# A mixed attention and recurrence network on one core: the two directions of the RWKV key products share a PSUM tile and one mask operation, and ScalarE makes all block copies of the triangular inverse

## The chip, the cores and the metric

The program runs on one core of a Trainium2 chip. TensorE (PE) does the matrix products, VectorE (DVE), ScalarE (ACT) and GpSimd (POOL) the elementwise work, and SyncE (SP) issues most transfers. The metric is the device time of one execution in microseconds, lower is better.

## The reference, cut to what matters

The whole network is two blocks of several layers (attention, a recurrent layer, feed-forward layers). The change touches one branch of the recurrent layer, an RWKV recurrence that runs over 512 tokens after 256 context tokens, once forwards and once backwards, for 8 heads of width 64, and the inverse that a later gated delta rule shares with it:

```python
def wkv_scan(s0, r, decay, k, v, kk, b, reverse, emit):
    xs = tuple(jnp.moveaxis(t, 1, 0) for t in (r, decay, k, v, kk, b))
    def step(s, inp):
        r_t, w_t, k_t, v_t, kk_t, b_t = inp
        sa = jnp.einsum('bhij,bhj->bhi', s, kk_t)
        s = s * w_t[:, :, None, :] - sa[..., None] * b_t[:, :, None, :] + v_t[..., None] * k_t[:, :, None, :]
        y = jnp.einsum('bhij,bhj->bhi', s, r_t) if emit else None
        return s, y
    s_final, ys = lax.scan(step, s0, xs, reverse=reverse)
    return s_final, (jnp.moveaxis(ys, 0, 1) if emit else None)
...
    for d in range(2):
        reverse = d == 1
        s_ctx, yc = wkv_scan(s0, rc, decay_c, k_c, vc, kkc, b_c, reverse, ctx_out)
        _, yl = wkv_scan(s_ctx, r, decay_l, k_l, v, kk, b_l, reverse, True)
```

## The kernel before, in words

**Windows.** The recurrence is done in chunks of 64 tokens. A window is two chunks in each direction; there are six windows, the first two over the context (they emit nothing) and four over the 512 tokens. Each window is prepared in two halves `h` of four heads (two head pairs `pr`), so there are 12 preparations: 4 of context windows and 8 of the others ("full" ones below; `lat` in the code).

**A preparation** (`prep`) calls `decays` for direction `d` = 0 and then 1, and `products` for 0 and then 1. `decays` computes the low-rank decay and rate into a PSUM tile `mm2` (L1153), and then by a chain over ScalarE, GpSimd and VectorE (`ta`, `kd`, `G`, `EP`) the operands `KR` (L1180) and `kT` (L1184). `products` multiplies the two (L1198). `kT` holds two blocks of 64 rows for each head, so that one product gives in one half of the PSUM rows the block `N` of the triangular system, and in the other the block `AK`; the half is swapped between the directions. For full windows the same product has 128 columns, and the second 64 give `DD`. ScalarE copies `N` out, in two pieces (L1210 and L1208), VectorE multiplies `AK` by a mask over 64 rows (L1211) and `DD` by a mask over 128 rows (L1213). Four PE transposes (L1219) and a ScalarE copy (L1220) make `kn`.

**PSUM.** The pool `mm2` has one buffer of two banks. Every `decays` and every `products` takes that one tile, so each waits until the last reader of the tile before it is done. In rows of the profile this tile is called `mm`, as is the tile of the large products.

**The inverse** (`unit_inverse`) is called once for each window and once in the gated delta rule. It inverts 32 x 32 blocks by a chain of 31 pairs of VectorE operations (L1331, L1333) between stream transposes (L1321, L1336, L1337), and then joins pairs of blocks by two rounds of 32 small products (L1351, then L1353). After each round the result is copied out of PSUM in two pieces of 32 rows: the first by ScalarE (L1361), the second by VectorE (L1359).

**The steps** (`rwkv_step`, L1387 to L1440) run the recurrence itself, 12 chunks by two halves.

**What sets the order.** A scheduler puts the instructions of the whole stage in a fixed order on each engine when the program is built; each engine then works through its list in that order and waits on semaphores. The large products that feed the rest of the layer (L114 to L116, three passes of 128 x 128 by up to 512 columns) are mixed into PE's list between the small ones. An instruction of fp32 operands of the small products appears in the trace as two MATMUL rows; in the order it is one.

Of the kernel before, what the change touches and what calls it, by code (L numbers as in the profile page):

```python
# [10 lines left out]
F32 = mybir.dt.float32  # L11
F32R = mybir.dt.float32r
AF = mybir.ActivationFunctionType
OP = mybir.AluOpType
# [1072 lines left out]
def rwkv(b, I, r, dram, late, rest, conv):  # L1087
# [11 lines left out]
    nc, tc = b.nc, b.tc  # L1099
# [6 lines left out]
    with ExitStack() as es:  # L1106
        P = lambda **kw: es.enter_context(tc.tile_pool(side="left", **kw))
        cp = P(name="rw_c", bufs=1)
        w3 = P(name="rw_3", bufs=4)
# [20 lines left out]
        mask, rsc = I["k_rwmask"], I["k_rwsc"]  # L1130
# [53 lines left out]
                nc.vector.tensor_mul(kT[:, :, :, q], chunks(src, d), chunks(G, 0))  # L1184
            return kT

        def products(o, d, h, kT):
            lat = o["w"] > 1
            kr, u0 = slice(64 * d, 64 * d + 64), 64 - 64 * d
            n = 128 if lat else 64  # L1190
            KR, AK = o["KR"][h][d], o["AK"][h]
# [9 lines left out]
            pv = ps[:, :, 0:4 * n].rearrange("p q (m x t) -> p q m x t", m=4, t=64)  # L1201
            by = lambda v: v.rearrange("p (m q) t -> p q m t", q=2)
            bc = lambda mk, k: mk[:, None, None, :].to_broadcast([k, 2, 4, 64])
            ms = slice(8 * h, 8 * h + 8)
            for blk in range(2):
                rw = slice(u0 + 32 * blk, u0 + 32 * blk + 32)
                if blk:
                    nc.scalar.activation(by(o["N"][rw, ms, 0:32]), pv[rw, :, :, 0, 32:64], AF.Copy, scale=-0.5)  # L1208
                else:
                    nc.scalar.activation(by(o["N"][rw, ms]), pv[rw, :, :, 0], AF.Copy, scale=-0.5)  # L1210
            nc.vector.tensor_tensor(by(AK[kr]), pv[kr, :, :, 0], bc(mask[kr, 0], 64), op=OP.mult)  # L1211
            if lat:
                nc.vector.tensor_tensor(by(o["DD"][h][:, d]), pv[:, :, :, 1], bc(mask[:, 1 + d], 128), op=OP.mult)  # L1213
            kn = w3.tile([128, 2, 2, 128], F32, name=f"kn{d}")
            p = b.psum(512, "tr")
            for c in range(2):
                for pr in range(2):
                    m = 2 * c + pr
                    nc.tensor.transpose(p[:, m * 128:m * 128 + 128], kT[:, pr, c].rearrange("p x t -> p (x t)"), b.ident)  # L1219
            nc.scalar.activation(kn.rearrange("p c r f -> p (c r f)"), p, AF.Copy, scale=rsc[:, d:d + 1])  # L1220
            o["kn"][h].append(kn)

        def window(w):
            return {"w": w, "KR": [[], []], "kn": [[], []], "PC": [], "AK": [], "DD": [],
# [2 lines left out]
        def prep(o, h):  # L1227
            o["PC"].append(w3.tile([128, 2, 2, 2], F32, name="PC"))
            o["AK"].append(w3.tile([128, 8, 64], F32, name="AK"))
            if o["w"] > 1:  # L1230
                o["DD"].append(w3.tile([128, 2, 8, 64], F32, name="DD"))
            kT = [decays(o, d, h) for d in range(2)]
            for d in range(2):
                products(o, d, h, kT[d])
# [79 lines left out]
def unit_inverse(b, wp, bp, N, u0, tag="tr"):  # L1314
# [3 lines left out]
    nc = b.nc  # L1318
# [7 lines left out]
    for s in range(31):  # L1326
# [16 lines left out]
    P1 = wp.tile([128, 16, 32], F32, name="inv_x")  # L1343
    for first in (True, False):
        p = b.psum(512, tag)
        for k in range(16):
            ps = slice(k * 32, k * 32 + 32)
            for u in u0:
                r0, r1 = slice(u, u + 32), slice(u + 32, u + 64)
                if first:  # L1350
                    mm(p[r1, ps], N[r0, k, 32:64], Tn[r0, k], start=True, stop=True, tile_position=(u, u + 32))  # L1351
                else:
                    mm(p[r0, ps], P1[r1, k], T[r1, k, 32:64], start=True, stop=True, tile_position=(u + 32, u))  # L1353
        pv = p.rearrange("p (m t) -> p m t", m=16)
        for j, u in enumerate(u0):
            rw = slice(u + 32, u + 64) if first else slice(u, u + 32)
            dst = P1[rw] if first else T[rw, :, 32:64]
            if j:
                nc.vector.tensor_copy(dst, pv[rw])  # L1359
            else:  # L1360
                nc.scalar.activation(dst, pv[rw], AF.Copy)  # L1361
    return T


# [1296 lines left out]
```

## Time and profile before

| | |
|---|---|
| time, median of 3 runs | 2864.5 us (2858.34 to 2864.9) |
| time of the profiled execution | 2864.4 us |
| its span, first to last instruction | 2861.5 us |
| mean granted TensorE clock | 0.951 |
| PE busy | 2645.9 us, 92% |
| VectorE busy | 1495.3 us, 52% |
| ScalarE busy | 1028.4 us, 36% |
| GpSimd busy | 503.8 us, 18% |

The preparations and steps of the recurrence lie between about 740 and 1230 us of the span. Busy time of PE counts pipelined instructions, so it says that PE had work, not that it ran at its peak. The granted clock is a share of 2.4 GHz.

### The profile page before, as it was taken

What the parts mean: (1) busy time and instruction counts of PE and PEld (TensorE: products, weight loads), DVE (VectorE), ACT (ScalarE), POOL (GpSimd) and SP (SyncE); (2) the same over time, 40 slices, a digit from 0 to 9 for tenths busy, and PEclk for the clock granted to TensorE, in tenths of its full rate; (3) what the DMA queues carried; (4) which work ended last, traced back from release to release, by engine and by line L of the source; (5) the groups of instructions that cost most, each with busy time, mean ns of one, the idle gap of its engine ahead of it and who ended that gap; (6) DMA issues with size and microseconds to landing.
All of it is one profiled execution on the core that took longest, in us unless ns stands there. A gap on an engine that the chain in (4) does not pass through costs nothing.

```text
span 2861.5 us, 43340 instructions
## 1 busy us (share of the span) xinstructions
PE 2645.9 (92%) x16642; PEld 2125.4 (74%) x16642; DVE 1495.3 (52%) x3219; ACT 1028.4 (36%) x2165; POOL 503.8 (18%) x803
## 2 busy tenths in 40 slices
PE   8998998989989889878999998999989999899998
PEld 5897445678767666658888877777868776888887
DVE  4144557736487888685344237762232566444423
ACT  4223335524344444223333224432222663323322
POOL 1011001222343332432000001311010344100000
PEclk9999899989899899988999998999987999999999
DMA  6111431142223332524333323232453315233332
GB/s 231 60 60 55 145 119 63 57 129 81 83 87 113 90 93 66 174 94 138 96 96 96 96 85 108 83 96 91 122 160 104 106 55 161 89 100 100 96 96 88
DMA packets 251018, 290.60 MB, mean 102 GB/s; under 512 B 17415, under 2 KB 197082, under 8 KB 250812
## 3 DMA queue, kind: packets, MB, share of 16 engines
q1 hardware_dynamic: 239292, 251.29, 28.4%
q0 software_dynamic: 10704, 33.41, 3.9%
q8 instruction: 131, 2.15, 0.3%
q10 hardware_dynamic: 816, 3.15, 0.3%
q14 instruction: 75, 0.61, 0.1%
HBM read 247.38 MB, written 35.68 MB: 99 GB/s over the span
## 4 chain that ended last, share of the span: by engine, by line
PE 71%; DVE 11%; issue 5%; POOL 5%; DMA 4%; ACT 3%; SPq 0%; DVEq 0%; POOLq 0%; ACTq 0%
PE mm L114 13%; PE mm L115 13%; PE mm L116 13%; PE gt L114 3%; PE gt L115 3%; PE gt L116 3%; PE ac L116 1%; PE ac L115 1%; PE ac L114 1%; PE ac L874 1%; PE fx L333 1%; PE ac L2053 1%; PE mm L813 1%; DVE wlo L109 1%; PE tr L857 1%
## 5 line engine op out<-in xcount | busy, mean ns | idle before, releaser
L109 DVE TENSOR_TENSOR wlo<-wraw,whi 128x512 fp32r<-128x512 f32 (+1 forms) x390 | 374.5, 961 | 690.1 <-ACT whi L108 683.3
L108 ACT ACTIVATE whi<-wraw 128x512 fp32r<-128x512 f32 (+1 forms) x390 | 323.7, 831 | 792.5 <-PE mm L115 224.3
L114 PE MATMUL mm<-hh,whi 128*128 128x512 f32 (+1 forms) x1024 | 384.0, 376 | 1.0 <-ACT hh L178 0.7
L115 PE MATMUL mm<-hl,whi 128*128 128x512 f32 (+1 forms) x1024 | 383.5, 375 | 0.0
L116 PE MATMUL mm<-hh,wlo 128*128 128x512 f32 (+1 forms) x1024 | 383.0, 374 | 0.1
L114 PEld LDWEIGHTS mm<-hh,whi 128*128 128x128 f32 x1024 | 193.8, 190 | 35.7 <-ACT hh L178 1.3
L116 PEld LDWEIGHTS mm<-hh,wlo 128*128 128x128 f32 x1024 | 193.5, 189 | 35.2 <-DVE wlo L109 1.2
L115 PEld LDWEIGHTS mm<-hl,whi 128*128 128x128 f32 x1024 | 193.9, 189 | 33.1
L114 PE MATMUL mm<-whi,mh 128*128 128x512 f32 (+1 forms) x480 | 172.4, 360 | 1.4 <-DVE th L2270 1.4
L115 PE MATMUL mm<-wlo,mh 128*128 128x512 f32 (+1 forms) x480 | 173.0, 360 | 0.1
L116 PE MATMUL mm<-whi,ml 128*128 128x512 f32 (+1 forms) x480 | 172.7, 360 | 0.0
L114 PE MATMUL gt<-hh,whi 128*128 128x512 f32 (+1 forms) x320 | 128.7, 402 | 7.0 <-ACT whi L108 6.4
L116 PE MATMUL gt<-hh,wlo 128*128 128x512 f32 (+1 forms) x320 | 128.3, 401 | 0.8 <-DVE wlo L109 0.8
L115 PE MATMUL gt<-hl,whi 128*128 128x512 f32 (+1 forms) x320 | 127.6, 399 | 0.0
L283 POOL TENSOR_TENSOR ss<-sq 128x1 f32<-128x1 f32 x8 | 1.6, 201 | 707.3 <-ACT th L277 707.3
L114 PE MATMUL mm<-lath,whi 128*128 128x512 f32 (+1 forms) x280 | 116.4, 417 | 0.1
L116 PE MATMUL mm<-lath,wlo 128*128 128x512 f32 (+1 forms) x280 | 113.7, 407 | 1.0 <-DVE wlo L109 1.0
L115 PE MATMUL mm<-latl,whi 128*128 128x512 f32 (+1 forms) x280 | 113.3, 405 | 0.4 <-DVE latl L179 0.4
L114 PEld LDWEIGHTS mm<-whi,mh 128*128 128x128 f32 x480 | 89.9, 188 | 15.8 <-DVE th L2270 1.8
L115 PEld LDWEIGHTS mm<-wlo,mh 128*128 128x128 f32 x480 | 90.1, 188 | 14.4 <-DVE wlo L109 0.8
L116 PEld LDWEIGHTS mm<-whi,ml 128*128 128x128 f32 x480 | 90.1, 188 | 13.8
L114 PEld LDWEIGHTS gt<-hh,whi 128*128 128x128 f32 x320 | 62.2, 194 | 21.7 <-ACT whi L108 7.4
(732 smaller groups left out, 5987.7 us busy)
## 6 DMA issues: line engine op xcount, KB each, us to landing
wraw<-in_ffn_w_gate SPq DMA_DIRECT2D x44, 512.0 KB, 3.5
wraw<-in_ffn_w_up SPq DMA_DIRECT2D x44, 512.0 KB, 3.6
wraw<-in_ffn_w_down SPq DMA_DIRECT2D x44, 512.0 KB, 3.7
wraw<-in_w_in SPq DMA_DIRECT2D x60, 256.0 KB, 2.8
wraw<-in_rec_w_in SPq DMA_DIRECT2D x58, 256.0 KB, 2.8
wraw<-in_attn_w_in SPq DMA_DIRECT2D x26, 512.0 KB, 3.7
ada_w<-in_rec_ada_w SPq DMA_DIRECT2D x24, 512.0 KB, 3.7
wraw<-in_w_branch_gate SPq DMA_DIRECT2D x48, 256.0 KB, 3.0
```

Of the source, the lines that this page charges most:

```text
L108: nc.scalar.activation(hi, raw, AF.Copy)
L109: self.weng.tensor_sub(lo, raw, hi.bitcast(F32))
L114: mm(out, lh, rh, start=start, stop=False)
L115: mm(out, lh, rl, start=False, stop=False)
L116: mm(out, ll, rh, start=False, stop=stop)
L283: nc.gpsimd.tensor_add(ss, sq[:, i, 0:1], sq[:, i, 1:2])
L333: nc.tensor.matmul(p[o:o + 32], self.cs[:, kk], w[:, k], start=kk < 4, stop=kk >= 4, tile_position=(0, o))
L813: nc.tensor.matmul(ps[p][:, o:o + n], qaT[heads[p], pr, 128 * i:128 * i + 128], ks[p], start=True, stop=True)
L857: nc.tensor.transpose(t[:, j * 128:j * 128 + 128], s[:, a:a + 128], b.ident)
L874: nc.tensor.matmul(o[heads[p], xs], va[rows, n, h * 64:h * 64 + 64], pT[rows, p, j, xs], start=j == 0, stop=j == nk - 1)
L2053: nc.tensor.matmul(o, r["v"][br][:, j], pT[br][:, j].rearrange("p a b -> p (a b)"), start=False, stop=br == 1 and j == i)
```

## The change

`products` now takes both directions at once. For the context part (`N` and `AK`) each 64-row block is a product of its own, put by `tile_position` into the PSUM half where it is wanted: the `N` blocks of both directions share one bank, the `AK` blocks the other. One mask operation of 128 rows then serves `AK` of both directions. `DD` gets a second `mm2` tile, taken after the first is released, with products of 64 columns. In the inverse ScalarE makes both copies of each round.

```diff
-        def products(o, d, h, kT):
+        def products(o, h, kT):
...
             ps = b.mm2.tile([128, 2, 512], F32, name="mm2")
             for c in range(2):
                 for pr in range(2):
-                    for q in range(2):
-                        qs = slice(64 * q, 64 * q + 64)
+                    for x in range(2):
+                        for d in range(2):
+                            for q in range(2):
+                                qs = slice(64 * q, 64 * q + 64)
+                                y = d ^ x
+                                m = 4 * x + 2 * c + pr
+                                nc.tensor.matmul(ps[64 * y:64 * y + 64, q, m * 64:m * 64 + 64], kT[d][qs, pr, c, y],
+                                                 KR[d][qs, pr, c, 0], start=True, stop=True,
+                                                 tile_position=(64 * q, 64 * y))
...
+            for d in range(2):
+                u0 = 64 - 64 * d
+                nc.scalar.activation(by(o["N"][u0:u0 + 32, ms]), pv[u0:u0 + 32, 1], AF.Copy, scale=-0.5)
+                nc.scalar.activation(by(o["N"][u0 + 32:u0 + 64, ms, 0:32]), pv[u0 + 32:u0 + 64, 1, :, :, 32:64],
+                                     AF.Copy, scale=-0.5)
+            nc.vector.tensor_tensor(by(AK), pv[:, 0], mask[:, 0][:, None, None, :].to_broadcast([128, 2, 4, 64]), op=OP.mult)
+            if lat:
+                ps = b.mm2.tile([128, 2, 512], F32, name="mm2")
+                for d in range(2):
+                    for c in range(2):
+                        for pr in range(2):
+                            for q in range(2):
+                                qs = slice(64 * q, 64 * q + 64)
+                                m = 4 * d + 2 * c + pr
+                                nc.tensor.matmul(ps[:, q, m * 64:m * 64 + 64], kT[d][qs, pr, c].rearrange("p x t -> p (x t)"),
+                                                 KR[d][qs, pr, c, 1], start=True, stop=True)
...
-                        nc.tensor.matmul(ps[:, q, m * n:m * n + n], kT[qs, pr, c].rearrange("p x t -> p (x t)"),
-                                         KR[qs, pr, c, 0:n // 64].rearrange("p x t -> p (x t)"),
-                                         start=True, stop=True)
...
-            nc.vector.tensor_tensor(by(AK[kr]), pv[kr, :, :, 0], bc(mask[kr, 0], 64), op=OP.mult)
...
-            dst = P1[rw] if first else T[rw, :, 32:64]
-            if j:
-                nc.vector.tensor_copy(dst, pv[rw])
-            else:
-                nc.scalar.activation(dst, pv[rw], AF.Copy)
+            nc.scalar.activation(P1[rw] if first else T[rw, :, 32:64], pv[rw], AF.Copy)
```

The scheduler's order changes with it. Line numbers of the changed kernel are its own: L1202 is the product for `N` and `AK`, L1221 that for `DD`, L1233 the transpose, L1212 and L1225 the masks, and lines behind `products` are higher by 8 to 12.

PE, first half of the first full window, before (the two L1198 are the products of direction 0 and of direction 1):

```order
L1198 MATMUL mm_8914<-KR_8876,kT_8879 128x128 x8
L1219 MATMUL tr<-ident,kT_8911 128x128 x4
L1259 MATMUL iv<-ident,vw 64x128 x4
L114 MATMUL mm<-lath,whi 128x512
L115 MATMUL mm<-latl,whi 128x512
L116 MATMUL mm<-lath,wlo 128x512
L114 MATMUL mm<-lath,whi 128x512
L115 MATMUL mm<-latl,whi 128x512
L1257 MATMUL iv<-ident,vpad 128x128 x4
L1387 MATMUL ru<-VU_9061,AK 64x64
L116 MATMUL mm<-lath,wlo 128x512
L1198 MATMUL mm_8934<-KR_8908,kT_8911 128x128 x8
```

The same place of the changed kernel, its beginning:

```order
L1202 MATMUL mm_8970<-KR_8932,kT_8935 64x64
L116 MATMUL mm<-lath,wlo 128x512
L1202 MATMUL mm_8970<-KR_8932,kT_8935 64x64
L114 MATMUL mm<-lath,whi 128x512
L1202 MATMUL mm_8970<-KR_8964,kT_8967 64x64
L115 MATMUL mm<-latl,whi 128x512
L1202 MATMUL mm_8970<-KR_8964,kT_8967 64x64
L116 MATMUL mm<-lath,wlo 128x512
L1202 MATMUL mm_8970<-KR_8932,kT_8935 64x64 x2
L1202 MATMUL mm_8970<-KR_8964,kT_8967 64x64 x2
L1202 MATMUL mm_8970<-KR_8932,kT_8935 64x64 x2
L114 MATMUL mm<-lath,whi 128x512
```

Two blocks of 8 products have become 32 smaller ones, and here nearly each of them stands alone between large products of another array shape; it goes on so to the 32nd.

PE, second half of the same window, before (L1219 is direction 1's transpose, L1198 its products):

```order
L1219 MATMUL tr<-ident,kT_9018 128x128 x4
L116 MATMUL mm<-lath,wlo 128x512
L1406 MATMUL ru<-VU_9076,kn_7950 64x64 x2
L1406 MATMUL ru<-VU_9084,kn_7969 64x64 x2
L1406 MATMUL ru<-VU_9076,kn_7950 64x64 x2
L1406 MATMUL ru<-VU_9084,kn_7969 64x64 x2
L114 MATMUL mm<-lath,whi 128x512
L115 MATMUL mm<-latl,whi 128x512
L1198 MATMUL mm_9041<-KR_9015,kT_9018 128x128 x8
```

The same place of the changed kernel, from the last of the `N` and `AK` products to those of `DD`:

```order
L1202 MATMUL mm_9108<-KR_9102,kT_9105 64x64 x2
L1233 MATMUL tr<-ident,kT_9105 128x128 x4
L1414 MATMUL ru<-VU_9194,kn_8018 64x64 x2
L1414 MATMUL ru<-VU_9202,kn_8025 64x64 x2
L1414 MATMUL ru<-VU_9194,kn_8018 64x64 x2
L1414 MATMUL ru<-VU_9202,kn_8025 64x64 x2
L115 MATMUL mm<-latl,whi 128x512
L116 MATMUL mm<-lath,wlo 128x512
L114 MATMUL mm<-lath,whi 128x512
L115 MATMUL mm<-latl,whi 128x512
L116 MATMUL mm<-lath,wlo 128x512
L114 MATMUL mm<-lath,whi 128x512
```

Here the small products stand in one block of 30. After these rows come two more large products and then the 16 `DD` products (L1221), which use the tile that the `AK` mask has to release first.

VectorE, end of the first window's inverse, before (from the two stream transposes on):

```order
L1336 STREAM_TRANSPOSE inv_n<-inv_x 128x32x16
L109 TENSOR_TENSOR wlo<-wraw,whi 128x512
L1337 STREAM_TRANSPOSE TT<-inv_n 128x2x16x32
L1359 COPY inv_x<-iv 32x512
L1321 STREAM_TRANSPOSE inv_n<-N 128x1024
L109 TENSOR_TENSOR wlo<-wraw,whi 128x512
L1359 COPY TT<-iv 32x16x32
```

The two copies L1359 have left VectorE's list in the changed kernel, and nothing stands in their place.

## Rows read from the trace of the kernel before

**Rows 1.** The page: busy time of each engine, share of the span, instructions.

```profile
PE 2645.9 (92%) x16642; PEld 2125.4 (74%) x16642; DVE 1495.3 (52%) x3219; ACT 1028.4 (36%) x2165; POOL 503.8 (18%) x803
```

**Rows 2.** Stretches: length, busy PE, weight loads, DVE, ACT, POOL; granted clock; DMA share, GB/s.

```profile
740.00:887.00 147.00, 132.52 (x1050) 102.97 (x1048) 109.31 (x263) 60.70 (x133) 57.99 (x96) 0.86 0.33 99
887.00:1030.00 143.00, 124.14 (x1333) 93.93 (x1328) 112.49 (x278) 63.62 (x145) 49.72 (x88) 0.90 0.31 90
1030.00:1145.00 115.00, 103.21 (x1347) 78.81 (x1348) 96.08 (x252) 50.35 (x115) 33.42 (x61) 0.99 0.27 78
```

**Rows 3.** Waits of PE, 740 to 1145 us: total, times, longest.

```profile
PE tr L1219 <- DVE kT L1184: 22.9, 13, 2.7
PE tr L1219 <- DVE inv_t L1331: 5.0, 2, 2.6
```

**Rows 4.** Timeline of PE: a block of 64 x 64 products, and what follows.

```profile
1002.89 0.68 PE L1387 MATMUL ru<-VU,AK 64*64 64x64 f32 x16
1003.50 0.33 PE L1392 MATMUL ru<-diag,KR 128*64 128x128 f32 x2
```

**Rows 5.** Timeline of PE: products L1198 of a context window, and what follows.

```profile
761.28 1.11 PE L1198 MATMUL mm<-KR,kT 64*128 64x64 f32 x16
762.32 0.50 PE L114 MATMUL mm<-lath,whi 128*128 128x512 f32 x1
```

**Rows 6.** Timeline of PE: products L1198 of a full window, and what follows.

```profile
1017.65 1.16 PE L1198 MATMUL mm<-KR,kT 64*128 64x128 f32 x16
1018.74 0.51 PE L114 MATMUL mm<-lath,whi 128*128 128x512 f32 x1
```

**Rows 7.** Timeline of PE: one 64 x 64 product (two rows) alone before large ones.

```profile
908.52 0.33 PE L1387 MATMUL ru<-VU,AK 64*64 64x64 f32 x2
908.77 0.51 PE L114 MATMUL mm<-lath,whi 128*128 128x512 f32 x1
909.12 0.39 PE L115 MATMUL mm<-latl,whi 128*128 128x512 f32 x1
```

**Rows 8.** Timeline of PE: the step from one large product to the next.

```profile
1043.34 0.40 PE L114 MATMUL mm<-lath,whi 128*128 128x512 f32 x1
1043.57 0.40 PE L115 MATMUL mm<-latl,whi 128*128 128x512 f32 x1
```

**Rows 9.** Groups by line and shape, 740 to 1230 us: busy, mean ns, idle before.

```profile
L1211 DVE TENSOR_TENSOR AK<-mm,k_rwmask 64x512 f32<-64x512 f32 x24 | 16.5, 687 | 14.7 <-ACT N L1208 14.5
L1210 ACT ACTIVATE N<-mm 32x512 f32<-32x512 f32 x24 | 14.1, 588 | 13.9 <-PE mm L1198 13.7
L1213 DVE TENSOR_TENSOR DD<-mm,k_rwmask 128x512 f32<-128x512 f32 x16 | 10.9, 682 | 0.1
L1208 ACT ACTIVATE N<-mm 32x256 f32<-32x256 f32 x24 | 9.0, 376 | 0.3
L1359 DVE COPY inv_x<-iv 32x512 f32<-32x512 f32 x6 | 4.1, 683 | 2.0 <-ACT inv_x L1361 2.0
```

**Rows 10.** Timeline, end of one full preparation and start of the next.

```profile
1020.75 0.59 ACT L1210 ACTIVATE N<-mm 32x512 f32<-32x512 f32 x1
1022.46 0.41 DVE L1184 TENSOR_TENSOR kT<-kd,G 128x256 f32<-128x256 f32 x1
1023.69 0.67 DVE L1213 TENSOR_TENSOR DD<-mm,k_rwmask 128x512 f32<-128x512 f32 x1
1031.49 0.69 DVE L1213 TENSOR_TENSOR DD<-mm,k_rwmask 128x512 f32<-128x512 f32 x1
1033.10 0.72 PE L1153 MATMUL mm<-lora,wu 32*128 32x128 f32 x8
```

**Rows 11.** Timeline, a round of the inverse: ScalarE, VectorE, then PE again.

```profile
835.18 0.59 ACT L1361 ACTIVATE inv_x<-iv 32x512 f32<-32x512 f32 x1 [2.32 <-PE iv L1351]
835.80 0.68 DVE L1359 COPY inv_x<-iv 32x512 f32<-32x512 f32 x1 [0.24 <-ACT inv_x L1361]
836.89 1.20 PE L1353 MATMUL iv<-TT,inv_x 32*32 32x32 f32 x64
```

More of the change, by code (lines that the diff above doesn't have):

```diff
@@ L1185, in decays @@
             return kT
-        def products(o, d, h, kT):
+        def products(o, h, kT):
             lat = o["w"] > 1
-            kr, u0 = slice(64 * d, 64 * d + 64), 64 - 64 * d
-            n = 128 if lat else 64
-            KR, AK = o["KR"][h][d], o["AK"][h]
+            AK, KR = o["AK"][h], o["KR"][h]
+            ms = slice(8 * h, 8 * h + 8)
             ps = b.mm2.tile([128, 2, 512], F32, name="mm2")
@@ L1202, in products @@
[L1202 to L1208, printed above, removed]
-                else:
-                    nc.scalar.activation(by(o["N"][rw, ms]), pv[rw, :, :, 0], AF.Copy, scale=-0.5)
@@ L1211, in products @@
-            nc.vector.tensor_tensor(by(AK[kr]), pv[kr, :, :, 0], bc(mask[kr, 0], 64), op=OP.mult)
[L1212 to L1219, printed above, removed]
@@ L1220, in products @@
-            nc.scalar.activation(kn.rearrange("p c r f -> p (c r f)"), p, AF.Copy, scale=rsc[:, d:d + 1])
-            o["kn"][h].append(kn)
+                    for x in range(2):
[7 more added lines that the diff above has]
+                                                 tile_position=(64 * q, 64 * y))
@@ new lines, in products @@
+            by = lambda v: v.rearrange("p (m q) t -> p q m t", q=2)
+            pv = ps.rearrange("p q (x m t) -> p x q m t", x=2, t=64)
+            for d in range(2):
[4 more added lines that the diff above has]
+            nc.vector.tensor_tensor(by(AK), pv[:, 0], mask[:, 0][:, None, None, :].to_broadcast([128, 2, 4, 64]), op=OP.mult)
@@ new lines, in products @@
+            if lat:
[8 more added lines that the diff above has]
+                                                 KR[d][qs, pr, c, 1], start=True, stop=True)
+                pv = ps.rearrange("p q (d m t) -> p d q m t", d=2, t=64)
+                for d in range(2):
+                    nc.vector.tensor_tensor(by(o["DD"][h][:, d]), pv[:, d], mask[:, 1 + d][:, None, None, :].to_broadcast([128, 2, 4, 64]),
+                                            op=OP.mult)
@@ new lines, in products @@
+            for d in range(2):
+                kn = w3.tile([128, 2, 2, 128], F32, name=f"kn{d}")
+                p = b.psum(512, "tr")
+                for c in range(2):
+                    for pr in range(2):
+                        m = 2 * c + pr
+                        nc.tensor.transpose(p[:, m * 128:m * 128 + 128], kT[d][:, pr, c].rearrange("p x t -> p (x t)"), b.ident)
+                nc.scalar.activation(kn.rearrange("p c r f -> p (c r f)"), p, AF.Copy, scale=rsc[:, d:d + 1])
+                o["kn"][h].append(kn)
@@ L1231, in prep @@
                 o["DD"].append(w3.tile([128, 2, 8, 64], F32, name="DD"))
-            kT = [decays(o, d, h) for d in range(2)]
-            for d in range(2):
-                products(o, d, h, kT[d])
+            products(o, h, [decays(o, d, h) for d in range(2)])
         def load_values(o):
@@ L1356, in unit_inverse @@
             rw = slice(u + 32, u + 64) if first else slice(u, u + 32)
-            dst = P1[rw] if first else T[rw, :, 32:64]
-            if j:
-                nc.vector.tensor_copy(dst, pv[rw])
-            else:
-                nc.scalar.activation(dst, pv[rw], AF.Copy)
+            nc.scalar.activation(P1[rw] if first else T[rw, :, 32:64], pv[rw], AF.Copy)
     return T
```

1 line of the change is left out of this document (removed).

## The prediction, written before the changed kernel was run

> **What bounds the kernel now.** I read the page first. TensorE is busy for 92% of the span [rows 1], so by and large what adds TensorE work adds time. But the change sits in one stage, and there I need the stage's own limit. The table of stretches shows it: from 740 to 1145 us, 405 us, TensorE is busy 132.52 + 124.14 + 103.21 = 359.9 us, 89%, and VectorE 109.31 + 112.49 + 96.08 = 317.9 us, 78%; ScalarE and GpSimd are under half [rows 2]. TensorE is idle for 405 - 359.9 = 45.1 us. Next I ask what it waits for: the table of waits puts 22.9 + 5.0 = 27.9 us of this on the transposes L1219, which stand in TensorE's list behind `kT`, the last product of VectorE's chain in `decays` [rows 3]. So the stage has two limits that take turns: mostly TensorE with its mixture of large and small products, and for about a tenth of the time the chain to `kT`. A saving on VectorE can win only in that tenth; more work on TensorE costs in the rest.
>
> **The change part by part.**
>
> *Products on TensorE.* A block of 16 rows of 64 x 64 products starts at 1002.89 and the next block at 1003.50: 0.61 / 16 = 0.038 us each [rows 4]. The old products load 64 x 128 weights: 1.04 / 16 = 0.065 us each with 64 columns [rows 5], and 1.09 / 16 = 0.068 us with 128 columns [rows 6]; twice the columns cost next to nothing, which the change gives away by splitting them. Each product is two rows. Before, a preparation has 2 directions x 8 products = 32 rows: 32 x 0.065 = 2.08 us in a context window, 32 x 0.068 = 2.18 us in a full one. After, `N` and `AK` are 32 products = 64 rows x 0.038 = 2.43 us, and in full windows `DD` is 16 products = 32 rows of the form of [rows 5], 2.08 us. A context preparation gains 0.35 us, a full one 2.43 + 2.08 - 2.18 = 2.33 us. Sum: 4 x 0.35 + 8 x 2.33 = **+20.0 us** of TensorE.
>
> *Changes of the array shape.* A single 64 x 64 product between large ones takes longer than its share of a block. From its start to the next product pass 0.25 us instead of 2 x 0.038 = 0.076, and the large product behind it takes 0.35 instead of the usual 0.23 [rows 7, 8]: 0.17 + 0.12 = 0.29 us for a visit, that is for two changes of shape. Counted over TensorE's order from the first preparation to the last step, the shape changes 302 times before and 373 after, and the increase lies between 128 x 128 and 64 x 64, most of it in the place that the order above shows, where the 32 products stand apart. 71 / 2 = 35.5 visits x 0.29 = **+10.3 us**. Had these visits the price of the surrounding blocks it would be 0, so 0 and 10.3 are the bounds; I take the whole, because the row is of just this form.
>
> *Masks and copies taken from VectorE.* L1211 falls from 24 to 12 at 0.687 us, -8.2 us. L1359 falls by two for each of seven inverses, 14 x 0.683 = -9.6 us, of which 12 (-8.2) lie in this stage [rows 9]. So VectorE loses 16.4 us here, 5% of its 317.9. It is worth time only where TensorE waits for VectorE, the 27.9 us above. Bounds: 0, if the chain to `kT` runs through GpSimd and ScalarE at the same pace as ever, and 16.4 + 2.0 us (the second is the idle time that VectorE spent in front of the copies for ScalarE) if every removed operation had stood in the chain. I take half of the 16.4, **-8 us**.
>
> *Copies added to ScalarE.* 14 at about 0.59 us (the first copy of a round in [rows 11]) are 8.3 us on an engine that is busy 174.7 of 405 us [rows 2]. In a round of the inverse the chain was ScalarE 835.18, VectorE 835.80 to 836.48, TensorE 836.89: 1.71 us [rows 11]. Two ScalarE copies in a row take 1.18 us and a hand-over of the same 0.4 us. 1.6 against 1.7 us, so nothing. The cover is ScalarE's idle time; without it the 8.3 us would stand in the chain.
>
> *The one `mm2` tile.* This is where a wait could be added: `DD` now takes a second tile, which opens only after four ScalarE copies and the `AK` mask, and behind it in TensorE's list stand the large products and the next `decays`. From the last `kT` to the next preparation's first product there were 1033.10 - 1022.87 = 10.2 us [rows 10]. They were that long because direction 0 was not out of the way early, as the code suggests: its ScalarE copy came at 1020.75 and its `DD` mask at 1023.69, after direction 1's `kT` [rows 10]. The new chain from `kT` on: products 2.43, ScalarE 2 x (0.588 + 0.376) = 1.93, mask 0.69, `DD` products 2.08, two masks 1.36, in all 8.5 us [rows 4, 5, 9], and some four hand-overs of 0.03 to 0.4 us [rows 11], so 9 to 10 us. I count **0**. If direction 0 is ready early, the old chain is 1.09 + 0.96 + 0.69 + 0.68 = 3.4 us and the new one longer by 5.1 us, for 8 full preparations +41 us: that is the upper bound.
>
> *Idle time that takes some of it.* The new products come behind the wait for `kT`, where TensorE has no gap to fill, but the large products that they displace move to other places, and some will fall in the 45.1 us of gaps. Between 0 and the whole 30.3 us; as the gaps are 11% of the stage, and large products are only moved a few places, I take **-6 us**.
>
> Sum: 20.0 + 10.3 - 8 + 0 - 6 = **+16.3 us**. The profiled execution took 2864.4 us and the median of the runs is 2864.5 us, so no correction is needed: **2881 us**, slower by 0.6%.
>
> A rule that would change the first term is in the Trainium skill, TensorEngine Tiling (Array Packing), section Key Properties: different tiles of the array can load weights and multiply in parallel. By it the four 64 x 64 positions through which the new loops go would overlap; the time that this gives is the third rival. The trace so far does not agree: the products of [rows 4] go through two different positions in turn and still take 0.038 us each.
>
> **The rivals.**
>
> *Faster: the stage is VectorE's and the chain's.* VectorE is at 78%, and in the place where TensorE waits it is VectorE that comes last [rows 2, 3]. If the 30.3 us of new TensorE work fit into the 45.1 us of gaps, and the 16.4 us of VectorE work come off the stage wholly or in part, the time is 2848 to 2856 us, say **2852 us**. It decides from the point where the gaps take more than about 22 of the 30.3 us. Against it: the gaps are single waits of at most 2.7 us in front of the transposes, not a stretch into which products could be moved.
>
> *No change: the two cancel.* The gaps take all of the new work and VectorE's relief gives nothing, or both terms are about 16 us: 2860 to 2870 us, **2865 us**. For it speaks that both terms are of one size.
>
> *The 64 x 64 products overlap in pairs.* Then they take 0.019 us a row, 1.22 instead of 2.43 us for a preparation, and the sum falls by 12 x 1.21 = 14.5 us, to **2866 us**. Against it stands [rows 4].
>
> *The tile `mm2` becomes the chain.* If in most full preparations direction 0 was done early, the 41 us come on top of part of the sum: some **2905 us**. Against it stands [rows 10].
>
> **How the numbers follow.** A difference under 0.3%, 8.6 us, could not be told from none in a measurement of this kernel. My forecast, slower by some 9 to 31 us (2873 to 2895), has a chance of 0.50; the long `mm2` chain 0.09; the overlapping products 0.07 and the cancelling 0.15, both within 0.3%; the faster case 0.19. So faster 0.19, same 0.22, slower 0.59. The range reaches from 2851, which leaves out about half of the faster case, to 2900, the forecast with no relief at all (2864.4 + 30.3 = 2895) and a little more for the granted clock of 0.86 to 0.90 in the first two stretches [rows 2], which leaves out the long chain: in all under 2 in 10 outside.
>
> **What would show it.** In the changed profile: TensorE's stage from the first `decays` to the last step is longer, with its gaps about as large as before; the new products take 0.038 us a row in blocks and about 0.29 us more for each that stands alone; VectorE's busy time is lower by some 18 us, and ScalarE's higher by 8; the transposes still wait for `kT`, a little less in total; the `DD` products wait hardly at all for the `AK` mask. I am wrong if the gaps before the transposes shrink by 20 us or more (faster or same), if the 64 x 64 rows come at 0.02 us (same), or if each `DD` block waits several microseconds for its tile (much slower).

## The result: slower by 0.7%

The kernel before took 2860.77 us (median of 6 runs, 2846.37 to 2864.9), the changed kernel 2879.83 us (median of 6, 2872.0 to 2884.33): ratio 1.0073, 95% interval 1.0045 to 1.0101. The profiled execution of the changed kernel took 2872.0 us, with a span of 2870.2 us.

Six executions are few. The experiments below had 77 executions of the kernel before run beside them (one slow one left out), with means of 2865.5, 2868.9 and 2865.7 us in three groups; the mean of the changed kernel, 2879.4 us, lies 10.5 to 13.9 us above them. That it is slower stands; whether by 13 or by 19 us does not.

The page of the changed kernel, busy time of each engine, to be held against [rows 1]:

```profile
PE 2655.6 (93%) x17282; PEld 2128.3 (74%) x17282; DVE 1483.0 (52%) x3193; ACT 1034.2 (36%) x2179; POOL 504.0 (18%) x803
```

TensorE is busy 9.7 us longer with 640 more instructions, VectorE 12.3 us shorter, ScalarE 5.8 us longer. The stage of the change, in the stretches of [rows 2] (the columns are the same):

```profile
740.00:887.00 147.00, 128.47 (x1244) 97.91 (x1242) 107.94 (x264) 63.95 (x143) 57.09 (x99) 0.91 0.35 106
887.00:1030.00 143.00, 126.44 (x1621) 94.22 (x1622) 102.44 (x257) 62.17 (x141) 49.87 (x84) 0.95 0.29 83
1030.00:1145.00 115.00, 104.15 (x1407) 81.19 (x1406) 86.06 (x227) 49.30 (x113) 33.65 (x55) 0.96 0.27 79
```

TensorE is idle for 405 - 359.06 = 45.9 us, against 45.1 before: the new products filled no gaps. VectorE has 296.4 us here, against 317.9. What TensorE waits for in the changed kernel, 740 to 1145 us (total, times, longest), beside [rows 3]:

```profile
PE mm L1202 <- DVE kT L1184: 10.0, 9, 1.9
PE tr L1233 <- DVE kT L1184: 7.1, 5, 2.1
...
PE mm L1153 <- DVE AK L1212: 2.1, 1, 2.1
```

The wait for `kT` now stands in front of the products L1202 and the transposes L1233, 17.1 us together instead of 22.9. So the picture of the stage is the one before, with some 6 us less of the wait that VectorE's relief was to shorten. The groups of the changed kernel, 740 to 1230 us, beside [rows 9]:

```profile
L1202 PE MATMUL mm<-KR,kT 64*64 64x64 f32 x768 | 27.7, 240 | 10.0 <-DVE kT L1184 10.0
L1221 PE MATMUL mm<-KR,kT 64*128 64x64 f32 x256 | 16.2, 275 | 1.6 <-DVE inv_t L1343 1.0 <-DVE AK L1212 0.6
L1212 DVE TENSOR_TENSOR AK<-mm,k_rwmask 128x512 f32<-128x512 f32 x12 | 8.2, 684 | 12.7 <-ACT N L1210 12.7
L1369 ACT ACTIVATE inv_x<-iv 32x512 f32<-32x512 f32 x12 | 7.1, 590 | 15.1 <-DVE TT L1349 10.7 <-PE iv L1363 4.3
L1369 ACT ACTIVATE TT<-iv 32x512 f32<-32x512 f32 x12 | 7.1, 589 | 6.1 <-PE iv L1365 6.0
```

A mask of 128 rows takes 684 ns, as one of 64 rows did (687 ns), so twelve masks are saved at full price. The `DD` products L1221 wait only 0.6 us for the `AK` mask, and one `decays` (L1153) 2.1 us: the second `mm2` tile is no chain. The old products L1198 stood in the same view with 23.5 + 10.9 = 34.4 us, the new ones have 27.7 + 16.2 = 43.9 us, 9.5 more; I had priced them at 20. The timeline of TensorE shows why:

```profile
758.74 0.33 PE L1202 MATMUL mm<-KR,kT 64*64 64x64 f32 x4
759.00 0.50 PE L114 MATMUL mm<-lath,whi 128*128 128x512 f32 x1
759.34 0.39 PE L115 MATMUL mm<-latl,whi 128*128 128x512 f32 x1
...
763.12 1.15 PE L1202 MATMUL mm<-KR,kT 64*64 64x64 f32 x60 [1.87 <-DVE kT L1184]
764.20 0.66 PE L1233 MATMUL tr<-ident,kT 128*128 128x128 f32 x4
...
904.93 2.00 PE L1221 MATMUL mm<-KR,kT 64*128 64x64 f32 x32 [0.19 <-DVE AK L1212]
906.87 0.66 PE L1269 MATMUL iv<-ident,vpad 128*128 128x128 f32 x4
```

Sixty rows of 64 x 64 products take 764.20 - 763.12 = 1.08 us, 0.018 us a row; eight of the nine blocks of sixty have just this (1.07 or 1.08), and the ninth, at a granted clock of 0.50, takes 1.90 us. The block in [rows 4] took 0.038 us a row. Both stand at a granted clock of 1.00, the 2.4 GHz level, so it is not the clock. A part is the length of the block: sixteen rows have the same beginning and end to pay as sixty. The rest can be seen in the kernel before, at a place where the rows of two lines come to be mixed, L1368 with the array positions (64, 64) and (0, 0) in turn and L1387 with (0, 64) and (64, 0):

```profile
883.23 0.28 PE L1368 MATMUL ru<-Rs,TT 64*64 64x64 f32 x3
883.29 0.22 PE L1387 MATMUL ru<-VU,AK 64*64 64x64 f32 x1
883.29 0.22 PE L1368 MATMUL ru<-Rs,TT 64*64 64x64 f32 x1
883.30 0.22 PE L1387 MATMUL ru<-VU,AK 64*64 64x64 f32 x1
883.35 0.22 PE L1368 MATMUL ru<-Rs,TT 64*64 64x64 f32 x1
```

While both lines take turns, four rows start within 0.01 us and the next four 0.06 us later, 0.015 us a row; of L1387 alone, behind this place, two rows start in each 0.058 us, 0.029 a row. But four positions go with two PSUM banks in both places (here each line has a tile of its own, the new products write two banks in turn), and L1387 alone writes one. No run changes the one without the other, so which of the two it takes is not shown.

The `DD` block has 1.94 / 32 = 0.061 us a row, a little under the 0.065 of [rows 5]. A visit, that is a few rows alone between large products, costs at first sight what [rows 7] said: 0.26 us to the next instruction, and 0.34 instead of 0.23 us for the large product behind it. But [rows 7] begins with the visit, and the large product in front of it takes longer too. In the first full preparation 26 visits of two rows (and one of twelve) follow each other with one large product between:

```profile
883.46 0.39 PE L115 MATMUL mm<-latl,whi 128*128 128x512 f32 x1
883.78 0.32 PE L1202 MATMUL mm<-KR,kT 64*64 64x64 f32 x2
884.03 0.51 PE L116 MATMUL mm<-lath,wlo 128*128 128x512 f32 x1
884.47 0.32 PE L1202 MATMUL mm<-KR,kT 64*64 64x64 f32 x2
```

The product in front takes 883.78 - 883.46 = 0.32 us, and one visit with one large product 884.47 - 883.78 = 0.69 us. The large product has 0.23 by itself and two rows in a block 0.04, so a visit costs 0.42 us and not 0.29. In the whole timeline the new products stand in 36 such short groups, of two or four rows.

### The profile page after: what moved, and what is told of

It reads as the page before. It is cut to its first block, busy times and chain, and to the rows that moved or that the text cites. A ratio compares the mean times of both kernels' runs of the same rounds, so it can differ in the third digit from the quotient of the medians.

```text
span 2870.2 us, 44573 instructions
## 1 busy us (share of the span) xinstructions
PE 2655.6 (93%) x17282; PEld 2128.3 (74%) x17282; DVE 1483.0 (52%) x3193; ACT 1034.2 (36%) x2179; POOL 504.0 (18%) x803
## 4 chain that ended last, share of the span: by engine, by line
PE 49%; DVE 5%; issue 3%; POOL 2%; DMA 1%; ACT 1%; SPq 0%; DVEq 0%; POOLq 0%; ACTq 0%
PE mm L116 10%; PE mm L115 10%; PE mm L114 10%; PE gt L114 3%; PE gt L115 3%; PE gt L116 3%; PE ac L2061 1%; PE mm L2034 1%; PE mm L1659 1%; PE tr L2051 1%; PE mm L1954 1%; POOL acc L2280 0%; DVE M L1671 0%; DVE wlo L109 0%; POOL rstd L126 0%
## 5 line engine op out<-in xcount | busy, mean ns | idle before, releaser
L114 PEld LDWEIGHTS mm<-hh,whi 128*128 128x128 f32 x1024 | 194.5, 191 | 35.5 <-ACT hh L178 1.3
L115 PEld LDWEIGHTS mm<-wlo,mh 128*128 128x128 f32 x480 | 90.1, 188 | 14.5 <-DVE wlo L109 0.8
```

The lines of the kernel that those rows point to most:

```text
L114: mm(out, lh, rh, start=start, stop=False)
L115: mm(out, lh, rl, start=False, stop=False)
```

## Twelve experiments

All were run beside the kernel before. The ratios carry intervals of about 0.3% each, since executions of one and the same kernel differ by about 1%. Each run also lists its granted TensorE clock, and that turned out to sort them: taken around each kernel's own mean, over the 200 runs of fourteen kernels that list it, the time falls by 2.17 us for each 0.001 of granted clock (correlation -0.91), and what is left scatters by 3.2 us instead of 7.6. So I split each difference of the mean times: "by clock" is the difference of the mean clocks times 2.17 us, "rest" is what remains at equal clock, within about 2 to 3.5 us (nearly 5 for the two masks). That the slope found among executions of one kernel also holds between kernels is an assumption.

| experiment | ratio, 95% interval | mean difference, us | mean clock, it / before | by clock | rest |
|---|---|---|---|---|---|
| products only | 1.0027 [1.0002, 1.0051] | +8.4 | 0.9542 / 0.9516 | -5.7 | +14.1 |
| copies only | 1.0044 [1.0014, 1.0074] | +13.1 | 0.9479 / 0.9516 | +7.9 | +5.2 |
| products twice | 1.0108 [1.0067, 1.0150] | +32.3 | 0.9493 / 0.9516 | +4.8 | +27.5 |
| old places | 1.0078 [1.0050, 1.0106] | +23.1 | 0.9489 / 0.9516 | +5.8 | +17.3 |
| two masks | 1.0086 [1.0052, 1.0119] | +27.0 | 0.9472 / 0.9497 | +5.6 | +21.4 |
| context only | 1.0041 [1.0014, 1.0068] | +11.7 | 0.9497 / 0.9497 | +0.1 | +11.6 |
| copies swapped | 0.9984 [0.9961, 1.0007] | -3.0 | 0.9503 / 0.9497 | -1.1 | -1.9 |
| copies on VectorE | 0.9966 [0.9942, 0.9990] | -8.4 | 0.9511 / 0.9497 | -3.0 | -5.5 |
| shared products, copies on VectorE | 1.0033 [1.0009, 1.0057] | +8.9 | 0.9519 / 0.9511 | -1.7 | +10.7 |
| kn twice | 1.0011 [0.9984, 1.0037] | +0.7 | 0.9515 / 0.9511 | -0.8 | +1.5 |
| masks twice | 1.0097 [1.0071, 1.0124] | +23.1 | 0.9462 / 0.9511 | +10.8 | +12.3 |
| N on VectorE | 1.0064 [1.0040, 1.0088] | +13.6 | 0.9480 / 0.9511 | +6.8 | +6.8 |

What the clock does to a block, the kernel before shows itself. TensorE's timeline has the same sixteen rows of L1198 as in [rows 6], where they took 1.16 us at a granted clock of 1.00, at another place with the clock at 0.50, the 1.2 GHz level:

```profile
985.45 2.08 PE L1198 MATMUL mm<-KR,kT 64*128 64x128 f32 x16
```

In the expectations theory A is the prediction's way of pricing (TensorE's time in full, VectorE's by half, ScalarE's at nothing), and theory B is that the cost comes from other work that the longer program moves to other places.

**Each half of the change alone.** The changed kernel with the old copies in the inverse:

```diff
-            nc.scalar.activation(P1[rw] if first else T[rw, :, 32:64], pv[rw], AF.Copy)
+            dst = P1[rw] if first else T[rw, :, 32:64]
+            if j:
+                nc.vector.tensor_copy(dst, pv[rw])
+            else:
+                nc.scalar.activation(dst, pv[rw], AF.Copy)
```

> The changed kernel, but with the inverse's copies shared between ScalarE and VectorE as before: only the products and the mask are changed. Theory A, added TensorE work in the stage: all of its 30 us stay, and the relief of VectorE is halved (8.2 of 16.4 us), so 4 us slower than the changed kernel: ratio to before about 1.008 to 1.009. Theory B, the loss comes from a later last inverse and last steps that fall behind the convolution at the end of the stage: about the changed kernel, 1.006 to 1.008, as the products are what moves the order.

And the other half, the kernel before with all of the inverse's copies on ScalarE:

```diff
-            if j:
-                nc.vector.tensor_copy(dst, pv[rw])
-            else:
-                nc.scalar.activation(dst, pv[rw], AF.Copy)
+            nc.scalar.activation(P1[rw] if first else T[rw, :, 32:64], pv[rw], AF.Copy)
```

> The kernel before, with all block copies of the inverse on ScalarE: only this part of the change. Theory A: VectorE loses 8.2 us in the stage, worth half where TensorE waits for it: 4 us faster, ratio about 0.9985. Rival, that VectorE's relief is worth all that it removes together with its waits: 10 to 15 us faster, ratio 0.995 to 0.9965. A third, that ScalarE's added 7 us stand in the chain: 1.002.

The products cost less than either theory said (1.0027), the copies cost where they were to give (1.0044). 0.27 + 0.44 = 0.71%, as the whole had, but each with about 0.3% to either side; at equal clock the halves are 14.1 + 5.2 = 19.3 us, and the changed kernel lies only 12 to 13 us above the 77 other executions of the kernel before. So that the halves add up is not shown. Why VectorE's relief gives nothing in the second half shows at one place of VectorE's timeline. In the kernel before:

```profile
985.14 0.68 DVE L1359 COPY TT<-iv 32x512 f32<-32x512 f32 x1 [2.02 <-ACT TT L1361]
988.58 0.69 DVE L1211 TENSOR_TENSOR AK<-mm,k_rwmask 64x512 f32<-64x512 f32 x1 [2.76 <-ACT N L1208]
```

and with the copies on ScalarE, the same place:

```profile
982.36 0.67 DVE L1213 TENSOR_TENSOR DD<-mm,k_rwmask 128x512 f32<-128x512 f32 x1
988.77 0.69 DVE L1211 TENSOR_TENSOR AK<-mm,k_rwmask 64x512 f32<-64x512 f32 x1 [5.74 <-ACT N L1208]
```

The copy is gone from VectorE, and the next instruction in its list, the `AK` mask, waits 5.74 instead of 2.76 us for `N`, to begin at the same moment. Over the stage the waits of `AK` for `N` grow from 14.5 to 22.6 us, by as much as the twelve copies took (8.2 us); with the copies on ScalarE the row of [rows 9] reads

```profile
L1211 DVE TENSOR_TENSOR AK<-mm,k_rwmask 64x512 f32<-64x512 f32 x24 | 16.5, 686 | 22.8 <-ACT N L1208 22.6
```


**The price of TensorE's work.** The kernel before with each product issued twice:

```diff
-                        nc.tensor.matmul(ps[:, q, m * n:m * n + n], kT[qs, pr, c].rearrange("p x t -> p (x t)"),
-                                         KR[qs, pr, c, 0:n // 64].rearrange("p x t -> p (x t)"),
-                                         start=True, stop=True)
+                        for _ in range(2):
+                            nc.tensor.matmul(ps[:, q, m * n:m * n + n], kT[qs, pr, c].rearrange("p x t -> p (x t)"),
+                                             KR[qs, pr, c, 0:n // 64].rearrange("p x t -> p (x t)"),
+                                             start=True, stop=True)
```

> The kernel before, with each product of KR and kT issued twice into the same place: about 26 us more TensorE work at the same places (8 x 2.18 + 4 x 2.08 us), in the same blocks, nothing else added, and the output is the same. Theory A: TensorE work in this stage costs most of its own time: 15 to 26 us slower, ratio 1.005 to 1.009. Rival, that the 45 us of gaps take it: under 5 us, ratio under 1.002.

27.5 us at equal clock, where these products are busy for 43.1 + 20.6 = 63.7 us instead of 34.4, 29.3 us longer: the work counts nearly in full, and the gaps take little of it, if any.

**The price of the other engines' work.** Each mask issued twice in the kernel before:

```diff
-            nc.vector.tensor_tensor(by(AK[kr]), pv[kr, :, :, 0], bc(mask[kr, 0], 64), op=OP.mult)
-            if lat:
-                nc.vector.tensor_tensor(by(o["DD"][h][:, d]), pv[:, :, :, 1], bc(mask[:, 1 + d], 128), op=OP.mult)
+            for _ in range(2):
+                nc.vector.tensor_tensor(by(AK[kr]), pv[kr, :, :, 0], bc(mask[kr, 0], 64), op=OP.mult)
+                if lat:
+                    nc.vector.tensor_tensor(by(o["DD"][h][:, d]), pv[:, :, :, 1], bc(mask[:, 1 + d], 128), op=OP.mult)
```

> The kernel before with every mask of AK and DD issued twice: 24 x 0.687 and 16 x 0.682 us, 27.4 us more of VectorE in the stage; TensorE and ScalarE as before. Theory P (half of VectorE's time counts): 13.7 us more, 1.0048. Theories S and L (VectorE's time is hidden here): 0.999 to 1.001.

At equal clock 12.3 us for 27.4, a share of 0.45: of added work half counts, as the prediction took it for work removed. Another 10.8 us go with a lower granted clock. The stretch from the first to the last decay product, the kernel before and then the doubled masks (columns as in [rows 2]):

```profile
754.10:1096.30 342.20, 300.22 (x3115) 232.29 (x3114) 269.63 (x660) 151.92 (x348) 129.39 (x224) 0.91 0.31 92
```

```profile
760.20:1113.60 353.40, 301.81 (x3133) 234.61 (x3134) 288.26 (x698) 154.61 (x352) 135.57 (x224) 0.91 0.31 90
```

TensorE's busy time hardly moves (+1.6 us), its idle time goes from 42.0 to 51.6 us. ScalarE, with one more activation for each `kn`:

```diff
-            nc.scalar.activation(kn.rearrange("p c r f -> p (c r f)"), p, AF.Copy, scale=rsc[:, d:d + 1])
+            for src in (kT.rearrange("p a b x t -> p (a b x t)"), p):
+                nc.scalar.activation(kn.rearrange("p c r f -> p (c r f)"), src, AF.Copy, scale=rsc[:, d:d + 1])
```

> The kernel before with 24 more ScalarE activations of 128x512 in the preparations (kn is written once from kT, then as before), about 0.69 us each, 16.6 us of ScalarE; nothing of the inverse is touched. Theory S: 12 to 17 us more, 1.004 to 1.006. Theory L (ScalarE costs only where the inverse waits for it) and theory P: 1.000.

1.0011, and 1.5 us at equal clock: theory S falls, ScalarE's busy time is free here. And work moved from ScalarE to VectorE, on top of the copies on VectorE:

```diff
-                    nc.scalar.activation(by(o["N"][rw, ms, 0:32]), pv[rw, :, :, 0, 32:64], AF.Copy, scale=-0.5)
+                    nc.vector.tensor_scalar_mul(by(o["N"][rw, ms, 0:32]), pv[rw, :, :, 0, 32:64], -0.5)
-                    nc.scalar.activation(by(o["N"][rw, ms]), pv[rw, :, :, 0], AF.Copy, scale=-0.5)
+                    nc.vector.tensor_scalar_mul(by(o["N"][rw, ms]), pv[rw, :, :, 0], -0.5)
```

> The kernel before with the inverse's copies and also the 48 evacuations of N on VectorE (a multiplication by -0.5 in place of ScalarE's scaled copy): 24 x 0.588 + 24 x 0.376 = 23.1 us less of ScalarE than with the inverse's copies alone on VectorE, some 28 us more of VectorE. Theory S: 23 us less than that kernel's 0.9966, about 0.989. Theory L: the same 0.9966. Theory P: 14 us more, 1.0015.

The groups of VectorE that this adds:

```profile
L1210 DVE TENSOR_SCALAR N<-mm 32x512 f32<-32x512 f32 x24 | 16.4, 683 | 7.0 <-PE mm L1198 6.6
L1208 DVE TENSOR_SCALAR N<-mm 32x256 f32<-32x256 f32 x24 | 10.2, 424 | 0.6
```

26.6 us more of VectorE bring 6.8 + 5.5 = 12.3 us at equal clock against the kernel with only the copies moved: 0.46, the same half (0.3 to 0.6 by the intervals). What ScalarE was spared shows nowhere.

**Where the copies stand.** Both of a round on VectorE, and the two exchanged:

```diff
-            if j:
-                nc.vector.tensor_copy(dst, pv[rw])
-            else:
-                nc.scalar.activation(dst, pv[rw], AF.Copy)
+            nc.vector.tensor_copy(dst, pv[rw])
```

> The kernel before, with both copies of each inverse round on VectorE: 12 copies of about 0.68 us more on VectorE (8.2 us), 12 of about 0.59 us less on ScalarE. Theory A: half of 8.2 us, ratio 1.0015. Theory S (two copies one behind the other cost the round their time, whichever engine makes them): as with both on ScalarE or more, 1.004 to 1.007. Theory R: 1.003 to 1.005.

```diff
-            if j:
+            if not j:
```

> The kernel before, with the two copies of each inverse round exchanged: the upper half's goes to VectorE and the lower half's to ScalarE. Each engine has the same number of the same copies, and they still run side by side. Theory A (work is what costs) and theory S (the copies' part costs because two copies stand one behind the other on one engine): 1.000, at most 0.998 to 1.002. Theory R (any redrawn order loses): 1.003 to 1.005.

The exchange changes nothing (0.9984, its interval holds 1), so an order that is merely redrawn doesn't have to cost: theory R falls in that form. All copies on VectorE are faster than the kernel before (0.9966), the opposite sign of all theories: 16.5 us of copies where 8.2 stood. In the kernel before, VectorE's copies into `TT` were held up by ScalarE's:

```profile
L1359 DVE COPY TT<-iv 32x512 f32<-32x512 f32 x6 | 4.1, 677 | 4.6 <-ACT TT L1361 4.6
```

with all of them on VectorE:

```profile
L1358 DVE COPY inv_x<-iv 32x512 f32<-32x512 f32 x12 | 8.3, 690 | 0.6 <-PE iv L1351 0.3
L1358 DVE COPY TT<-iv 32x512 f32<-32x512 f32 x12 | 8.2, 684 | 5.4 <-PE iv L1353 5.2
```

VectorE's idle time in front of its copies hardly changes: 2.0 [rows 9] + 4.6 = 6.6 us before, ended by ScalarE, and 0.6 + 5.4 = 6.0 us now, ended by TensorE. But the two copies of a round did not run side by side before either, as the expectation of the exchanged copies took it: in each of the 14 rounds, the gated delta rule's two among them, the second begins only after the first has ended, 1.30 us for both in [rows 11], and two copies on VectorE take about 1.37. So a round is hardly longer. That could account for a cost of next to nothing; why it gains 5.5 us stays open. The changed kernel with its copies on VectorE:

```diff
-            nc.scalar.activation(P1[rw] if first else T[rw, :, 32:64], pv[rw], AF.Copy)
+            nc.vector.tensor_copy(P1[rw] if first else T[rw, :, 32:64], pv[rw])
```

> The changed kernel, but all 24 block copies of the inverses on VectorE (none on ScalarE). Theory P (the prediction's: VectorE time counts half, ScalarE's copies nothing): 24 x 0.68 = 16.4 us of VectorE more than the changed kernel, half of it 8 us: ratio to the kernel before 1.010. Theory S (ScalarE's time is what costs in this stage, about 1 us for each copy, VectorE's nothing) and theory L (only the wait for ScalarE inside the inverse costs): the changed kernel's 1.0073 less 0.0044 and less 0.0034, about 0.9995; from the products alone (1.0027) less 0.0034 the same.

1.0033, under the changed kernel's 1.0073, but their intervals overlap; beside the products-only kernel (1.0027) it is no gain, though copies on VectorE gained 0.34% in the kernel before. So the two halves don't simply add here.

**Places, context windows, the mask.** The stage's work is placed by its share of the whole length, which the change makes longer; this kernel maps the places back:

```diff
-            return tc.high_priority(offset=int(tc.cur_priority - p0 - x * (p1 - p0)))
+            was = [0, 890, 1347, 1814, 2353, 2892, 3268, 3456]
+            now = [0, 950, 1469, 1998, 2599, 3200, 3576, 3764]
+            t = x * 3456
+            j = min(max(k for k in range(8) if was[k] <= t), 6)
+            t = now[j] + (t - was[j]) * (now[j + 1] - now[j]) / (was[j + 1] - was[j])
+            return tc.high_priority(offset=int(tc.cur_priority - p0 - t))
```

> The changed kernel, but the convolution and the other work that is placed at fractions of the recurrence's instruction count stand at the same point of the loop as before (the 308 more instructions had moved these points by about 30 instructions). Theory A: no difference to the changed kernel, ratio to before about 1.007. Theory B, the last steps lose to the convolution because of the moved places: 10 us come back, ratio 1.003 to 1.004.

Nothing comes back (1.0078): the moved places are not the cause. The new products in the four context preparations alone:

```diff
+            if o["w"] > 1:
                 for d in range(2):
                     products(o, d, h, kT[d])
+            else:
+                shared(o, h, kT)
```

(`shared` is the changed kernel's `products`)

> The kernel before, with the products and the mask shared by both directions in the four context preparations alone; the eight full preparations and the inverse's copies as before. Theory A: TensorE gains 4 x 0.35 = 1.4 us, VectorE loses 4 x 0.68 = 2.7 us, of which half counts: 2864 us, ratio 1.000; with the 5 to 9 us by which the trace of the changed kernel has the second inverse start earlier, kept to the end, 0.997. Theory R (any redrawn order loses): 1.003 to 1.005.

1.0041, and +11.6 us at equal clock, where TensorE's term gives about nothing and VectorE has 2.7 us less: a miss for theory A. The four preparations alone cost about as much as all twelve (+14.1). TensorE's timeline shows where: the steps' own products, mostly blocks of sixteen rows in the kernel before, are cut into lone pairs here (L1421 is the old L1368):

```profile
880.35 0.32 PE L1421 MATMUL ru<-Rs,TT 64*64 64x64 f32 x2
880.61 0.50 PE L115 MATMUL mm<-latl,whi 128*128 128x512 f32 x1
881.03 0.33 PE L1421 MATMUL ru<-Rs,TT 64*64 64x64 f32 x2
```

Counted in the traces from the first decay product to the last step, the array's shape changes 308 times in the kernel before, 380 in the changed kernel, 392 with the products only and 389 here, but 309 with the copies only and 315 with the copies swapped. 81 more changes are 40.5 visits of 0.42 us, +17.0 us; the products of four context preparations take 4 x (1.15 - 2.08) = -3.7 us, half of the masks is -1.4: by this estimate +11.9 us, and 11.6 were measured. So what costs is not that the order is new, as theory R had it, but that it cuts blocks of small products apart. This is worked out from the traces; no run takes the visits away and leaves the rest.

Last, the changed kernel with its mask in two halves again:

```diff
-            nc.vector.tensor_tensor(by(AK), pv[:, 0], mask[:, 0][:, None, None, :].to_broadcast([128, 2, 4, 64]), op=OP.mult)
+            for d in range(2):
+                kr = slice(64 * d, 64 * d + 64)
+                nc.vector.tensor_tensor(by(AK[kr]), pv[kr, 0], mask[kr, 0][:, None, None, :].to_broadcast([64, 2, 4, 64]), op=OP.mult)
```

> The changed kernel with its one 128-row mask of AK split again into two of 64 rows (twelve more VectorE instructions of about 0.68 us, 8.2 us of VectorE in the stage; TensorE's and ScalarE's work as in the changed kernel). Theory A (VectorE time in this stage is worth about half of itself, as the prediction counted it): the ratio to the kernel before goes from 1.0073 to about 1.0087 (4 us more); were VectorE's time worth all of itself, 1.010. Theory R (the parts are not priced by their work, but any new order that the scheduler draws loses 0.3 to 0.5% against the kernel before, whose order is a favourable draw): 1.005 to 1.010 with no relation to the masks, so 1.007 is as likely as 1.009.

1.0086 against the changed kernel's 1.0073: as theory A says, but each interval reaches 0.3% to either side of a difference of 0.13%, so this decides nothing.

## Why the prediction came out right, step by step

The time, 2881 against 2879.83 us, is right, and so are the sign and the likeliest case. Of the terms, four were wrong in size, and they cancelled. That the time came out is luck.

*Products on TensorE, +20.0 us: the step that failed.* It rested on 0.038 us a row from [rows 4]. The new products take 0.018, so 64 rows take 1.15 instead of 2.43 us, 12 x 1.28 = 15.4 us less; the `DD` rows take 1.94 instead of 2.08 us, 8 x 0.14 = 1.1 us less. The term should have been about +3.5 us. The rival of the overlapping pairs came true in the rate that it named. The evidence against it, [rows 4], was of another kind than I thought: there the products alternate between two positions, (0, 64) and (64, 0), and write one bank, in blocks of sixteen rows; the new loops go through all four positions and write two banks, mostly in blocks of sixty. The Trainium skill, TensorEngine Tiling (Array Packing), Key Properties, says that different tiles can load weights and multiply in parallel. The trace agrees for the four positions (0.018 us a row against 0.038 for two); that two take 0.038 does not speak against it, as the prediction took it, since no row of a single position stands beside it. That TensorE's work counts nearly in full, the doubled products bear out.

*Changes of the array shape, +10.3 us.* The number stands: 36 lone groups in the trace, and 380 - 308 = 72 more changes of shape (35.5 visits were counted). The price does not: a visit costs 0.42 us instead of 0.29, because the large product in front of it is slowed too, and [rows 7] starts behind that. 36 x 0.42 = 15.1 us, about 5 us more than predicted. The context windows alone bear this price out (11.9 us estimated, 11.6 measured); no run took the visits away by themselves.

*Gaps, -6 us.* Failed: TensorE's gaps are as long as before (45.9 against 45.1 us), and the doubled products cost 27.5 us for 29.3 us of busy time.

*VectorE's relief, half of it.* The half is right for work added in the preparations, 0.45 and 0.46 in two runs; by it the masks would give about -4 us, which no run shows by itself. It is wrong for the copies: what they left on VectorE became a wait for `N`.

*Copies on ScalarE, 0 us.* ScalarE's time is free (`kn` twice), but the copies' half as a whole, -4 us by the prediction, was +5.2 us at equal clock and +13.1 in the mean. In its profile the stretch from the first to the last decay product reads:

```profile
751.50:1102.90 351.40, 311.44 (x3116) 239.66 (x3115) 264.09 (x651) 157.89 (x358) 131.35 (x225) 0.88 0.30 89
```

TensorE is idle 40.0 us, less than the 42.0 of before; it is busy 11.2 us longer, with as many rows (3116 against 3115) at a granted clock of 0.88 instead of 0.91. So in this execution the loss is TensorE running slower, not waiting longer. Its twelve runs have the lower clock too (0.9479 against 0.9516). Whether the copies cost as much in the changed kernel is not shown, as the halves need not add up.

*The sum, set right:* 3.5 + 15.1 - 4 = +14.6 us at equal clock, and some 5 us more if the copies cost here what they cost alone, where the prediction had 16.3. Measured are 19.1 us between the medians, and 12 to 13 us at equal clock against the 77 other executions. The products were put 16.5 us too high; the visits (5), the gaps (6) and the relief by the copies (4) together 15 us too low. By the prediction's own test (rows at 0.02 us mean no change) it should have been wrong; the dearer visits, the gaps that took nothing and the copies that gave nothing made up for it.

*The single `mm2` tile, 0 us:* right, 0.6 us of waits for the `AK` mask in front of the `DD` products and 2.1 us once in front of a `decays`.

**What stays open.** Why the copies on ScalarE alone cost 5 us at equal clock and lower the clock besides, and why copies on VectorE gain 5.5 us; what the one mask is worth by itself; whether the fast rows need four positions or two banks; and whether the whole change costs 13 or 19 us. The products alone have 84 more changes of shape, 42 visits: 3.5 + 17.6 - 4 = 17 us by the same estimate, and 14.1 were measured, so the estimate is good to some 3 us.

The kernel before with all of the inverse's copies on VectorE beats both: 2860.17 us against 2867.98 us of the kernel before beside it.

## What to carry to other kernels

Price an operation by a row that goes through the same positions of the array and the same banks, in blocks as long, not only by one of the same shape: here a 64 x 64 row took 0.018 or 0.038 us. Look where the new order cuts blocks of small products into lone pairs between large ones, and price such a visit from the start of the large product in front of it: here 0.42 us each, the largest term of the sum. Ask of an operation that you take away what stands next in its engine's list: if that waits for someone else, the saving only lengthens the wait. And compare kernels at equal granted clock where each run lists it: it took four fifths of the variance out of the times here, and tells work apart from a slower TensorE.

## What the hardware showed unexpectedly

- 64 x 64 products: 0.018 us a row in blocks of sixty through four positions and two banks, 0.038 in blocks of sixteen that alternate between two positions and write one bank, both at 2.4 GHz.
- Two rows of 64 x 64 alone between two 128 x 128 products of 512 columns cost 0.42 us at 2.4 GHz: they take 0.25 us to the next instruction, and the products in front and behind are slowed by about 0.1 us each.
- VectorE's mask of 128 x 512 takes 684 ns, of 64 x 512 687 ns: 64 rows more cost nothing.
- Two copies out of one bank by ScalarE and VectorE did not run side by side: in all 14 rounds the second began only after the first had ended (0.03 us later in [rows 11]), ScalarE's first in the kernel before, VectorE's first with the two exchanged. Whether the chip or the program's semaphores ask for that, no run here shows.
- Executions of one kernel differ by about 1%, and the time goes with their granted clock: 2.17 us less for each 0.001 more.
